# Diagonal blocks fetched by transfers, key and value banks evacuated by ScalarE, and the block inversion placed two projections later in a one-core encoder layer

## The chip, the core and the metric

The kernel runs on one core of a Trainium2 chip. The core has five instruction queues that run beside each other: PE (matrix products, with its weight loads PEld), DVE (vector engine), ACT (scalar engine: copies, exponentials and other table functions), POOL (GpSimd) and SP, which here only issues DMA transfers. Each queue is in order; engines wait for each other by semaphores. The metric is the device time of one execution in microseconds, lower is better.

## What is computed

One encoder layer on 1024 tokens of width 1024, in float32:

```python
xn = _rmsnorm(h, norm_mix_w[l])
proj = xn @ w_in[l]
q_a, k_a, v_a, qkv_g, z_g, a_g, b_g = jnp.split(proj, SPLIT_POINTS, axis=-1)
attn = _windowed_gqa(q_a, k_a, v_a, band_bias, in_window, attn_sink[l])   # 8 heads, 2 key/value heads
gdn = _gdn_mixer(qkv_g, z_g, a_g, b_g, conv_w[l], ...)                    # 4 heads, both directions
h = h + jnp.concatenate([attn, gdn], axis=-1) @ w_out[l]
h = h + jnp.square(jax.nn.relu(_rmsnorm(h, norm_ffn_w[l]) @ w_ffn_in[l])) @ w_ffn_out[l]
```

Inside the gated delta rule, each chunk, head and direction needs the inverse of a unit triangular matrix built of key products, decays and a factor:

```python
a_mat = jnp.where(strict, beta[..., :, None] * kk * decay, 0.0)
t_mat = lax.linalg.triangular_solve(eye + a_mat, jnp.broadcast_to(eye, a_mat.shape), left_side=True, lower=True)
```

The kernel uses chunks of 128 tokens, so there are 8 chunks, 4 heads and 2 directions, 64 matrices of 128 x 128.

## The kernel before

Every large product is done as three matmuls of 128 x 128 by 128 x 512 (`mm3`, L134): each operand is split into a high part (a cast on ACT, L123) and a low part (a subtraction, on POOL as a rule, L124). A projection of 128 output columns for 512 tokens is one `gemm` (L267): 24 matmuls into one of the four PSUM banks of the tag psA. `pair` (L273) walks two column tiles by two token halves, and splits the weights of a tile just ahead of its first use.

The program is written as generators. `weave` (L56) merges two streams by the costs that they yield; the order of the program is then handed to a scheduler which gives each engine its queue. An instruction traced inside `issue_after(x)` (or `behind([...])`) is put behind x, if it runs on x's engine. Tiles come from pools by tag: pg (24 buffers), pt (12), wh and wl (3 each), sc (4), dbl (2), psB (four PSUM banks) and so on; a tile waits until the buffer that it takes is free.

The stage that the change touches is the first woven one in `phases` (L1410). One stream runs 28 projections: eight of the gated heads' values with their convolutions (`proj_conv`), eight of the gate z with a Silu on ACT (L473), four of attention's keys and values and eight of its queries (`proj_attn`). The other stream runs these steps:

- `prep` (L643): for each of 8 chunks, key products (`gg`, L650) and key by query products (`kq`, L652) on PE; for each direction the decay's exponent on PE (L657, L658), its exponential on ACT (L662), the matrix `at` on DVE (L666), the copies of its four 32 x 32 diagonal blocks into `diag` on ACT (L671, 64 in all), the store of `at` to DRAM (`atd`, L673), and the decayed query products (L674) with their store.
- `eliminate` (L678): two transposes of `diag` (L683) and 31 rounds of two operations (L692, L694) invert all 256 diagonal blocks at once, on DVE.
- `diag_blocks` (L698): four transposes on DVE (L703, L704) give `ct` and `ctt`.
- `invert` (L708) for the first two pairs of chunks: products on PE with `at` read back from DRAM (L727), first in blocks of 32 (L756, L769, L773), then of 64 (L798, L809), and copies between them on ACT (L737 for direction 0, L743, L759, L800) and DVE (L737 for direction 1, L783, L788, L812).

In `proj_attn` DVE takes each key and value bank out of PSUM (L491) and writes zeros into half of the low keys `kl` (L486). For a key bank SP issues two transfers that swap its halves of 64 partitions (L494, L495), ACT writes the high keys (L497, L498) and POOL the low ones (L499). A value bank is transposed on PE and copied by DVE (L503). A query bank is scaled by DVE (L509), split by ACT (L510) and POOL (L511), and stored.

Then `bias_table` (L533) issues 16 transfers of the relative bias from ACT's queue (L541) into buffers that the projection's operands leave. The second woven stage starts attention (`attn_scores`: products L556 and L557, the sum with the bias and the maximum on DVE L558, the exponential on ACT L570, the division L577, transposes L589) beside the inversion of the last two pairs of chunks and the scans. That inversion's 32-blocks are copied into one tile, `later`, by 16 copies on ACT (L743).

Of the kernel before, what the change touches and what calls it, by code (L numbers as in the profile page):

```python
# [17 lines left out]
P = 128  # L18
# [60 lines left out]
class Block:  # L79
# [187 lines left out]
    def gemm(self, ws, xs, pstag):  # L267
        ps = self.ps(pstag)
        for k in range(NK):
            self.mm3(ps, ws[0][:, k, :], ws[1][:, k, :], xs[k][:, 0], xs[k][:, 1], k == 0, k == NK - 1)  # L270
        return ps

    def pair(self, raws, order=None):  # L273

        ws = []
        for half in range(2):
            for i in range(2):
                if half == 0:
                    ws.append(self.split_w(raws, lambda r: r[:, :, i * P:(i + 1) * P]))
                yield i, half, self.gemm(ws[i], self.xt[half], "psA")  # L280
# [186 lines left out]
    def proj_z(self):  # L467
        nc = self.nc
        for p in range(2):
            raws = self.load_w(self.w_cols(self.io["w_in"][0], C_Z + 256 * p, 256))  # L470
            for i, half, ps in self.pair(raws):
                z = self.pt()
                nc.scalar.activation(out=z, in_=ps, func=AF.Silu)  # L473
# [3 lines left out]
    def proj_attn(self):  # L477
# [7 lines left out]
        for v, o in enumerate((up, lo)):  # L485
            nc.vector.tensor_copy(out=self.kl[v][o, :], in_=self.zero[o, :].to_broadcast([64, SEQ]))  # L486
        self.va = self.pg((P, NT, P))
        for i, half, ps in self.pair(raws):
            tok = slice(half * HALF, (half + 1) * HALF)
            t = self.pt()  # L490
            self.taken = nc.vector.tensor_copy(out=t, in_=ps).ins  # L491
            if i == 0:
                swap = self.pt()
                nc.sync.dma_start(out=swap[up, :], in_=t[lo, :])  # L494
                nc.sync.dma_start(out=swap[lo, :], in_=t[up, :])  # L495
                for v, (r, o) in enumerate(((lo, up), (up, lo))):
                    nc.scalar.copy(out=self.kh[v][r, tok], in_=t[r, :])  # L497
                    nc.scalar.copy(out=self.kh[v][o, tok], in_=swap[o, :])  # L498
                    nc.gpsimd.tensor_tensor(out=self.kl[v][r, tok], in0=t[r, :], in1=self.kh[v][r, tok].bitcast(F32),  # L499
                                            op=ALU.subtract)  # L500
            else:
                pv = self.transposed(t, 0)
                nc.vector.tensor_copy(out=self.va[:, 4 * half:4 * half + 4, :], in_=pv)  # L503
            yield 5.2
        for kv in range(2):
            raws = self.load_w(self.w_cols(w, C_AQ + 256 * kv, 256))
            for i, half, ps in self.pair(raws):
                q, qh = self.pt(), self.pt(dt=F32R)
                self.taken = nc.vector.tensor_scalar(out=q, in0=ps, scalar1=0.125, scalar2=None, op0=ALU.mult).ins  # L509
                self.copied_q.append(nc.scalar.copy(out=qh, in_=q).ins)  # L510
                nc.gpsimd.tensor_tensor(out=q, in0=q, in1=qh.bitcast(F32), op=ALU.subtract)  # L511
# [131 lines left out]
    def prep(self):  # L643
        nc = self.nc
        self.diag = [self.pg((P, 32, 32)) for _ in range(2)]
        for c in range(NT):
            sl = slice(c * P, (c + 1) * P)
# [5 lines left out]
            for d in range(2):  # L653
# [15 lines left out]
                for q in range(4):  # L669
                    r = slice(32 * q, 32 * q + 32)  # L670
                    nc.scalar.copy(out=self.diag[d][r, :, 4 * c:4 * c + 4].rearrange("p i h -> p h i"),  # L671
                                   in_=at[r, :, r])
                nc.sync.dma_start(out=self.atd[c, :, d], in_=at)  # L673
                nc.vector.tensor_tensor(out=dec, in0=dec, in1=kq, op=ALU.mult)  # L674
# [3 lines left out]
    def eliminate(self):  # L678
# [3 lines left out]
        for d in range(2):  # L682
            nc.vector.transpose(out=m[:, d].rearrange("p a b -> p b a") if d else m[:, d], in_=self.diag[d])  # L683
# [23 lines left out]

    def invert(self, tt, steps):  # L708
# [10 lines left out]
        for i in steps:  # L719
            ns = slice(8 * i, 8 * i + 8)  # L720
            at = []
            if i == 2:
                later = self.wl((P, 2, 8, 64), F32)
            both = self.dbl((P, 2, 2, GH, P))
            for d in range(2):
                a = both[:, d]
                nc.sync.dma_start(out=a, in_=self.atd[2 * i:2 * i + 2, :, d].rearrange("c p h x -> p c h x"))  # L727
# [11 lines left out]
            def pieces(t64, ns):  # L739
                for d in range(2):  # L740
                    for q in sub[d]:
                        c = slice(32 * (q % 2), 32 * (q % 2) + 32)
                        nc.scalar.copy(out=t64[blk(q), :, c], in_=ct[d][blk(q), :, ns].rearrange("p x n -> p n x"))  # L743

# [3 lines left out]
            if i == 2:  # L748
                for j in range(2):
                    pieces(later[:, j], slice(8 * (i + j), 8 * (i + j) + 8))  # L750
            px = self.ps("psB", (P, 8, 32))
            for n in range(8):
                for j in range(2):
                    for d in range(2):
                        s, e = pairs[d][j]
                        nc.tensor.matmul(px[blk(e), n, :], at[d][blk(s), n, blk(e)], ct[d][blk(s), :, 8 * i + n],  # L756
# [757 lines left out]
```

## Time and profile before

| | us |
|---|---|
| median of 3 runs (lowest, highest) | 1209.62 (1207.96, 1210.77) |
| the profiled execution | 1209.66 |
| its span, first to last instruction | 1207.9 |
| PE, DVE, ACT and POOL busy in the span | 1170.3, 855.2, 611.1, 560.2 |
| mean granted clock of PE | 0.993 |

Busy times are those of instructions; waiting, and issuing a DMA, do not count. An answer in order of time has the start, the time from the first to the last of the instructions merged in the line, the engine (with a q: its queue, as in a DMA's issue), the line of the kernel, the operation with its tiles, the count, and in brackets the idle time before it and what ended it. An answer of waits has the total, the count and the longest. A row of one line of the kernel has the count, the shortest, median and longest instruction in ns, and the first and last start. A row of DMA issues has the count, the size of each and the median time from issue to landing. A group of instructions has busy time, the mean ns of one, and the idle time ahead of them with what ended it.

### The profile page before, as it was taken

How to read it: one execution, taken by the hardware profiler on the slowest of the kernel's cores; microseconds unless marked ns; L12 is line 12 of the kernel's file. 1: busy time of each engine (PE TensorE's matmuls, PEld its weight loads, DVE VectorE, ACT ScalarE, POOL GpSimd, SP SyncE). 2: the span in 40 equal slices, each digit the busy share in tenths (PEclk: the TensorE clock that was granted, in tenths of full speed). 3: DMA queues.
4: the chain of work that ended last, by engine and by line, in shares of the span. 5: the costliest groups of instructions: out<-in, count | busy, mean ns of one | idle time of the engine just before them, and what ended most of it. 6: DMA issues, size and time to landing. Idle time of an engine off the chain costs nothing. (4 is left out here: it accounts for less than half of the span.)

```text
span 1207.9 us, 18456 instructions
## 1 busy us (share of the span) xinstructions
PE 1170.3 (97%) x6482; PEld 958.9 (79%) x6482; DVE 855.2 (71%) x1484; ACT 611.1 (51%) x1332; POOL 560.2 (46%) x469
## 2 busy tenths in 40 slices
PE   6999999899989999999999999999999999999997
PEld 5788878687768778888888888888878888888885
DVE  4676667894299996687864545454588896987976
ACT  6455597425475752134755545454646444344443
POOL 5354211234422235143856354454546565555695
PEclk9999999899999999999999999999999999999999
DMA  6124344533555567323253444444789535443323
GB/s 248 53 92 144 93 162 161 174 117 103 202 183 163 180 215 265 130 89 123 64 176 136 157 143 153 140 151 158 246 290 304 185 105 174 131 159 113 105 88 139
DMA packets 121773, 187.62 MB, mean 155 GB/s; under 512 B 11059, under 2 KB 64432, under 8 KB 121681
## 3 DMA queue, kind: packets, MB, share of 16 engines
q1 hardware_dynamic: 104020, 155.20, 39.1%
q10 hardware_dynamic: 17661, 31.24, 6.8%
q8 instruction: 51, 0.84, 0.3%
q14 instruction: 41, 0.34, 0.1%
HBM read 122.39 MB, written 63.49 MB: 154 GB/s over the span
## 5 line engine op out<-in xcount | busy, mean ns | idle before, releaser
L136 PE MATMUL psA<-pg,wh 128*128 128x512 f32 x416 | 165.2, 398 | 2.1 <-ACT pt L473 2.1
L138 PE MATMUL psA<-pg,wl 128*128 128x512 f32 x416 | 164.7, 396 | 0.0
L137 PE MATMUL psA<-pg,wh 128*128 128x512 f32 x416 | 164.3, 395 | 0.0
L124 POOL TENSOR_TENSOR wl<-wr,wh 128x512 fp32r<-128x512 f32 x44 | 66.7, 1537 | 157.2 <-ACT wh L123 127.9
L1247 DVE TENSOR_TENSOR pg<-pg 128x512 fp32r<-128x512 f32 x112 | 124.4, 1146 | 11.8 <-ACT pg L1246 11.8
L124 POOL TENSOR_TENSOR wh<-wr,wh 128x512 fp32r<-128x512 f32 x32 | 47.4, 1499 | 137.1 <-ACT wh L123 137.1
L1158 ACT ACTIVATE pt<-pt 128x512 f32<-128x512 f32 x64 | 40.3, 632 | 122.7 <-DVE pt L1148 122.7
L136 PE MATMUL psA<-pg,pg 128*128 128x512 f32 x256 | 98.9, 392 | 0.9 <-DVE pg L1294 0.9
L137 PE MATMUL psA<-pg,pg 128*128 128x512 f32 x256 | 99.4, 391 | 0.1
L138 PE MATMUL psA<-pg,pg 128*128 128x512 f32 x256 | 99.2, 389 | 0.0
L136 PEld LDWEIGHTS psA<-pg,wh 128*128 128x128 f32 x416 | 78.8, 189 | 19.5 <-ACT pt L473 2.4
L137 PEld LDWEIGHTS psA<-pg,wh 128*128 128x128 f32 x416 | 78.8, 189 | 18.1 <-issue 0.9
L138 PEld LDWEIGHTS psA<-pg,wl 128*128 128x128 f32 x416 | 78.7, 189 | 16.8
L124 POOL TENSOR_TENSOR pg<-wr,pg 128x512 fp32r<-128x512 f32 x48 | 73.1, 1555 | 38.9 <-ACT pg L123 38.9
L1246 ACT CAST pg<-pg 128x512 fp32r<-128x512 f32 x112 | 66.8, 621 | 39.3 <-DMA pg<-sd 33.1
L137 PE MATMUL psB<-pg,pg 128*128 128x512 f32 x192 | 74.9, 390 | 0.8 <-POOL pg L124 0.7
L136 PE MATMUL psB<-pg,pg 128*128 128x512 f32 x192 | 74.7, 389 | 0.0
L138 PE MATMUL psB<-pg,pg 128*128 128x512 f32 x192 | 74.7, 389 | 0.0
L1148 DVE TENSOR_TENSOR pt<-psB,pt 128x512 f32<-128x512 f32 x39 | 26.9, 690 | 59.8 <-PE psB L138 41.3
L123 ACT CAST wh<-wr 128x512 fp32r<-128x512 f32 x76 | 43.6, 623 | 48.0 <-PE psA L137 27.7
L1148 DVE TENSOR_TENSOR pt<-psA,pt 128x512 f32<-128x512 f32 x39 | 26.7, 689 | 49.4 <-PE psA L138 33.8
L136 PEld LDWEIGHTS psA<-pg,pg 128*128 128x128 f32 x256 | 48.2, 188 | 12.3 <-DVE pg L1294 2.2
(405 smaller groups left out, 3231.5 us busy)
## 6 DMA issues: line engine op xcount, KB each, us to landing
sd<-pt ACTq DMA_DIRECT2D x112, 256.0 KB, 2.1
pg<-sd SPq DMA_DIRECT2D x112, 256.0 KB, 2.8
wr<-in_w_ffn_in SPq DMA_DIRECT2D x32, 512.0 KB, 3.7
wr<-in_w_in SPq DMA_DIRECT2D x22, 512.0 KB, 5.2
pg<-in_x SPq DMA_DIRECT2D x16, 512.0 KB, 6.1
wr<-in_w_ffn_out SPq DMA_DIRECT2D x16, 512.0 KB, 4.6
sc<-kvd SPq DMA_DIRECT2D x14, 512.0 KB, 4.7
kvd<-pt SPq DMA_DIRECT2D x16, 256.0 KB, 2.5
```

The costliest lines, as they stand in the source:

```text
L123: a = nc.scalar.copy(out=h, in_=raw)
L124: b = (eng or nc.gpsimd).tensor_tensor(out=l, in0=raw, in1=h.bitcast(F32), op=ALU.subtract)
L136: nc.tensor.matmul(ps, wh, xh, start=first, stop=False, skip_group_check=onto)
L137: nc.tensor.matmul(ps, wh, xl, start=False, stop=False, skip_group_check=onto)
L138: return nc.tensor.matmul(ps, wl, xh, start=False, stop=last, skip_group_check=onto)
L1148: self.added = self.nc.vector.tensor_tensor(out=out, in0=in0, in1=in1, op=ALU.add).ins
L1158: self.nc.scalar.activation(out=c, in_=c, func=AF.Relu)
L1246: nc.scalar.copy(out=s[:, 0], in_=raw)
L1247: v.tensor_tensor(out=s[:, 1], in0=raw, in1=s[:, 0].bitcast(F32), op=ALU.subtract)
```

## The change

- The store `atd` has direction and partition outermost. The diagonal blocks of chunks 0 to 5 are fetched from it by 16 DMAs, eight ahead of chunk 5 (chunks 0 to 3) and eight ahead of chunk 7 (chunks 4 and 5). Those of chunk 6 are still copied by ACT, those of chunk 7 are moved by eight DMAs straight out of `at`. `diag` has its two inner axes exchanged, so both transposes read with a stride; they are put behind the last L674.
- ACT evacuates the key and value banks, transposed values and all, fills the zeros and issues the swaps. The low keys are subtracted on POOL behind the split of a query. The first weight split of this part is put behind the first Silu.
- The stream of the inversion gets a step of cost 24 ahead of it, which moves it in program order, and its first products are put behind the last matmul of the projection traced before them (`projected`).
- The 16 copies into `later` move ahead of the bias transfers, with an Exp of one column behind a query's split, which brings the Exp table.

```diff
     def gemm(self, ws, xs, pstag):
...
-            self.mm3(ps, ws[0][:, k, :], ws[1][:, k, :], xs[k][:, 0], xs[k][:, 1], k == 0, k == NK - 1)
+            m = self.mm3(ps, ws[0][:, k, :], ws[1][:, k, :], xs[k][:, 0], xs[k][:, 1], k == 0, k == NK - 1)
+        self.projected = m.ins
...
-    def pair(self, raws, order=None):
+    def pair(self, raws, after=()):
...
-                    ws.append(self.split_w(raws, lambda r: r[:, :, i * P:(i + 1) * P]))
+                    with self.behind(() if i else after):
+                        ws.append(self.split_w(raws, lambda r: r[:, :, i * P:(i + 1) * P]))
...
     def proj_attn(self):
...
-        for v, o in enumerate((up, lo)):
-            nc.vector.tensor_copy(out=self.kl[v][o, :], in_=self.zero[o, :].to_broadcast([64, SEQ]))
+        late = []
         self.va = self.pg((P, NT, P))
-        for i, half, ps in self.pair(raws):
+        for i, half, ps in self.pair(raws, self.gated[:1]):
...
-            self.taken = nc.vector.tensor_copy(out=t, in_=ps).ins
+            copied = nc.scalar.copy(out=t, in_=ps)
             if i == 0:
                 swap = self.pt()
-                nc.sync.dma_start(out=swap[up, :], in_=t[lo, :])
-                nc.sync.dma_start(out=swap[lo, :], in_=t[up, :])
+                nc.scalar.dma_start(out=swap[up, :], in_=t[lo, :])
+                nc.scalar.dma_start(out=swap[lo, :], in_=t[up, :])
+                late.append((t, tok))
+                if half == 0:
+                    with self.tc.issue_after(copied.ins):
+                        for v, o in enumerate((up, lo)):
+                            nc.scalar.copy(out=self.kl[v][o, :], in_=self.zero[o, :].to_broadcast([64, SEQ]))
...
-                nc.vector.tensor_copy(out=self.va[:, 4 * half:4 * half + 4, :], in_=pv)
+                nc.scalar.copy(out=self.va[:, 4 * half:4 * half + 4, :], in_=pv)
...
-                nc.gpsimd.tensor_tensor(out=q, in0=q, in1=qh.bitcast(F32), op=ALU.subtract)
+                low = nc.gpsimd.tensor_tensor(out=q, in0=q, in1=qh.bitcast(F32), op=ALU.subtract)
+                if late:
+                    t, tok = late.pop(0)
+                    for v, r in enumerate((lo, up)):
+                        with self.tc.issue_after(low.ins):
+                            nc.gpsimd.tensor_tensor(out=self.kl[v][r, tok], in0=t[r, :],
+                                                    in1=self.kh[v][r, tok].bitcast(F32), op=ALU.subtract)
...
     def prep(self):
...
+            if c in (5, NT - 1):
+                a, b = (0, 4) if c == 5 else (4, 6)
+                for d in range(2):
+                    for q in range(4):
+                        r = slice(32 * q, 32 * q + 32)
+                        nc.sync.dma_start(out=self.diag[d][r, 4 * a:4 * b, :],
+                                          in_=self.atd[d, r, a:b, :, r].rearrange("p c h x -> p (c h) x"))
...
-                for q in range(4):
+                nc.sync.dma_start(out=self.atd[d, :, c], in_=at)
+                for q in range(4 if c > 5 else 0):
                     r = slice(32 * q, 32 * q + 32)
-                    nc.scalar.copy(out=self.diag[d][r, :, 4 * c:4 * c + 4].rearrange("p i h -> p h i"),
-                                   in_=at[r, :, r])
-                nc.sync.dma_start(out=self.atd[c, :, d], in_=at)
-                nc.vector.tensor_tensor(out=dec, in0=dec, in1=kq, op=ALU.mult)
+                    if c == 6:
+                        nc.scalar.copy(out=self.diag[d][r, 4 * c:4 * c + 4, :], in_=at[r, :, r])
+                    else:
+                        nc.sync.dma_start(out=self.diag[d][r, 4 * c:4 * c + 4, :], in_=at[r, :, r])
+                self.decayed = nc.vector.tensor_tensor(out=dec, in0=dec, in1=kq, op=ALU.mult).ins
...
     def eliminate(self):
...
-            nc.vector.transpose(out=m[:, d].rearrange("p a b -> p b a") if d else m[:, d], in_=self.diag[d])
+                nc.vector.transpose(out=m[:, d].rearrange("p a b -> p b a") if d else m[:, d],
+                                    in_=self.diag[d].rearrange("p x i -> p i x"))
...
+    def pieces_behind(self):
+        self.later = self.wl((P, 2, 8, 64), F32)
+        for i in range(2):
+            self.pieces(self.later[:, i], 2 + i)
+        with self.tc.issue_after(self.copied_q[-4]):
+            self.nc.scalar.activation(out=self.small((P, 1), 1, "table"), in_=self.eps, func=AF.Exp)
...
     def invert(self, tt, steps):
...
+                        with self.behind([self.projected] if i == 0 else []):
+                            nc.tensor.matmul(px[blk(e), n, :], at[d][blk(s), n, blk(e)], ct[d][blk(s), :, 8 * i + n],
+                                             start=True, stop=True)
...
     def phases(self):
...
-                  (chain(self.prep(), self.eliminate(), self.diag_blocks(), self.invert(tt, (0, 1))), 100.0)))
+                  (chain(self.prep(), self.eliminate(), self.diag_blocks(), iter((24.0,)),
+                         self.invert(tt, (0, 1))), 100.0)))
+        self.pieces_behind()
         self.bias_table()
```

`pieces` is the former inner function of `invert`, now a method with the same copies.

More of the change, by code (lines that the diff above doesn't have):

```diff
@@ L472, in proj_z @@
                 z = self.pt()
-                nc.scalar.activation(out=z, in_=ps, func=AF.Silu)
+                self.gated.append(nc.scalar.activation(out=z, in_=ps, func=AF.Silu).ins)
                 nc.sync.dma_start(out=self.zd[2 * p + i, :, half * HALF:(half + 1) * HALF], in_=z)
@@ L681, in eliminate @@
         m, t = self.dbl((P, 2, 32, 32)), self.dbl((P, 2, 32, 32))
-        for d in range(2):
-            nc.vector.transpose(out=m[:, d].rearrange("p a b -> p b a") if d else m[:, d], in_=self.diag[d])
+        with self.tc.issue_after(self.decayed):
+            for d in range(2):
+                nc.vector.transpose(out=m[:, d].rearrange("p a b -> p b a") if d else m[:, d],
+                                    in_=self.diag[d].rearrange("p x i -> p i x"))
         nc.gpsimd.memset(t.rearrange("p d a b -> p (d a b)"), 0.0)
@@ L706, in diag_blocks, with pieces @@
             yield 2.4
+    def pieces(self, t64, i):
+        for d, sub in enumerate(((0, 1), (3, 2))):
+            for q in sub:
+                r, c = slice(32 * q, 32 * q + 32), slice(32 * (q % 2), 32 * (q % 2) + 32)
+                self.nc.scalar.copy(out=t64[r, :, c],
+                                    in_=self.ct[d][r, :, 8 * i:8 * i + 8].rearrange("p x n -> p n x"))
+    def pieces_behind(self):
[4 more added lines that the diff above has]
+            self.nc.scalar.activation(out=self.small((P, 1), 1, "table"), in_=self.eps, func=AF.Exp)
     def invert(self, tt, steps):
@@ L726, in invert @@
                 a = both[:, d]
-                nc.sync.dma_start(out=a, in_=self.atd[2 * i:2 * i + 2, :, d].rearrange("c p h x -> p c h x"))
+                nc.sync.dma_start(out=a, in_=self.atd[d, :, 2 * i:2 * i + 2])
                 at.append(flat(a))
@@ L737, in diagonal @@
                     nc.vector.tensor_copy(out=out, in_=src) if d else nc.scalar.copy(out=out, in_=src)
[L739 to L743, printed above, removed]
             if i == 2:
@@ L776, in invert @@
                 t64 = self.pt((P, 8, 64))
-                pieces(t64, ns)
+                self.pieces(t64, i)
             else:
-                t64 = later[:, i - 2]
+                t64 = self.later[:, i - 2]
             for d in range(2):
@@ L802, in invert @@
             if i < 2:
-                with self.behind([self.taken]):
+                with self.behind(self.taken):
                     diagonal(1)
```

15 lines of the change are left out of this document (4 added, 11 removed).

## The prediction, made before the change was run

> **What bounds the kernel now.** I read the page first, then the waits of PE, then the windows and the order of time where PE waits. The profiled execution took 1209.66 us, 1.8 us of it outside the span, and its span is
>
> ```profile
> span 1207.9 us, 18456 instructions
> ...
> PE 1170.3 (97%) x6482; PEld 958.9 (79%) x6482; DVE 855.2 (71%) x1484; ACT 611.1 (51%) x1332; POOL 560.2 (46%) x469
> ```
>
> PE is the bound: it is idle for 1207.9 - 1170.3 = 37.6 us. An edit pays only where PE waits or runs at a lower clock, and costs only where it makes PE wait. The waits of PE from 144 to 222 us, the stage in which `prep` runs beside the projections (the longest three), and from 325 to 345 us, the start of attention (the longest two):
>
> ```profile
> PE psB L424 <- DVE pt L674: 1.7, 1, 1.7
> PE psB L652 <- ACT pt L662: 0.6, 1, 0.6
> PE psB L424 <- ACT pt L662: 0.6, 2, 0.4
> ```
>
> ```profile
> PE psB L769 <- ACT pt L759: 1.9, 1, 1.9
> PE psA L589 <- DVE wr L577: 1.2, 1, 1.2
> ```
>
> The windows give the clock of the place where the first ones lie (columns: length, then busy us of PE, PEld, DVE, ACT, POOL, then the granted clock):
>
> ```profile
> 210.00:220.00 10.00, 7.39 (x46) 5.46 (x45) 8.16 (x17) 9.79 (x27) 6.64 (x5) 1.00 0.75 238
> 220.00:230.00 10.00, 7.85 (x24) 6.13 (x23) 9.15 (x18) 3.70 (x6) 0.98 (x2) 0.66 0.80 279
> ```
>
> ACT is busy for 9.79 of 10 us, PE is idle for 2.61 + 2.15 = 4.76 us in these 20 us, and the second ten run at a mean clock of 0.66. PE in order of time, round the hole:
>
> ```profile
> 214.31 0.39 PE L137 MATMUL psA<-pg,wh 128*128 128x512 f32 x1
> 214.54 0.39 PE L138 MATMUL psA<-pg,wl 128*128 128x512 f32 x1
> ...
> 222.31 0.80 PE L136 MATMUL psA<-pg,wh 128*128 128x512 f32 x1 [2.15 <-ACT pt L473]
> ...
> 227.60 0.51 PE L136 MATMUL psA<-pg,wh 128*128 128x512 f32 x1
> ```
>
> At full clock one projection matmul follows the next by 0.23 us (first two rows). From 222.31 to 227.60, 12 of them take 5.29 us, where 12 x 0.23 = 2.76 were due: 2.53 us lost to the clock, behind a hole whose own idle time is 4.76 us. And ACT, which ends the hole:
>
> ```profile
> 213.92 2.18 ACT L662 ACTIVATE pt<-psB,ngc 128x128 f32<-128x128 f32 x8
> 215.94 1.66 ACT L671 COPY pg<-pt 32x128 f32<-32x128 f32 x4
> 217.63 1.14 ACT L123 CAST wh<-wr 128x512 fp32r<-128x512 f32 x2
> 218.67 1.68 ACT L671 COPY pg<-pt 32x128 f32<-32x128 f32 x4
> 220.37 1.28 ACT L473 ACT_TABLE_LOAD   x1
> 221.66 0.60 ACT L473 ACTIVATE pt<-psA 128x512 f32<-128x512 f32 x1
> ```
>
> The Silu of the first gate projection (L473), which frees the PSUM bank that PE waits for, stands behind the exponentials, two groups of diagonal copies (L671), a weight cast (L123) and its table load. ACT's queue is the cause, not PE's work.
>
> **The diagonal copies become transfers.** All the copies are
>
> ```profile
> L671 ACT COPY pg<-pt x64: 398/418/438, 148.2 to 219.9; 32x128 f32<-32x128 f32 x64
> ```
>
> Chunk 6 keeps 8 of 64. 56 x 0.418 = 23.4 us leave ACT. What that is worth is read at the hole. Behind the last exponential (213.92 + 2.18 = 216.1) the two groups of copies (1.66 + 1.68) and the cast (1.14, put behind the first Silu by the new edge in `pair`) go; the Silu's table load starts at about 216.1 and the first Silu ends near 216.1 + 1.28 + 0.60 = 218.0, where it ended near 222.3. That is 4.3 us at the least, with no operation of an earlier chunk moved. Earlier chunks lose their copies too, so the exponentials come earlier as well and the 0.6 us at L652 goes. Upper bound: all of 0.64 + 4.76, plus 2.53 of the clock, 7.9 us. What is late next is DVE's L674, which frees the PSUM banks of the four groups of transposes (L424); for that I keep 1.0 us of idle time. I take -6.9 us. From below: -4.3 if the clock falls as before.
>
> On this the Trainium skill, page "TensorE: Matmul & The Clock Gate", Part 1, has a rule: a window of about 3.4 us of idle PE halves the clock. The longest wait here is 2.15 us, and the clock fell all the same; by the page's Part 4 transposes do not count as busy in the same way, and from the last projection matmul to the next there are 7.8 us. By that reading a hole of 3.4 us is still enough, and the sum would be 2.5 us worse.
>
> **The transfers themselves.** 24 DMAs of 128-byte runs join SP's queue: eight ahead of chunk 5 (512 runs each), eight ahead of chunk 7 (256), eight of chunk 7 itself out of SBUF (128). Behind them on SP stand the writes of the later chunks and the next weight loads, none of which PE needs for some ten us. The first two batches wait for writes that landed chunks ago. Only the last lie on a path, that of the elimination. For their landing the nearest rows:
>
> ```profile
> pt<-pt SPq DMA_DIRECT2D x4, 128.0 KB, 4.6
> ...
> wr<-in_w_in SPq DMA_DIRECT2D x1, 64.0 KB, 4.8
> ```
>
> An SBUF to SBUF transfer lands after 4.6 us, one with 1024 runs of 64 bytes after 4.8 us. I take 4.7, from 2.5 to 8. The page "DMA: Bandwidth & Descriptors" of the Trainium skill (Specifications) says that runs under 512 bytes miss the line rate; the 4.8 us row, with shorter runs than any here, shows no long delay, so the term stays.
>
> The elimination on DVE now:
>
> ```profile
> 220.38 1.91 DVE L683 STREAM_TRANSPOSE dbl<-pg 128x1024 f32<-128x1024 f32 x1 [0.93 <-ACT pg L671]
> 222.39 0.26 DVE L692 TENSOR_TENSOR pt<-dbl,dbl 128x62 f32<-128x62 f32 x1
> 222.56 2.47 DVE L464 TENSOR_TENSOR pt<-psB,irk 128x512 f32<-128x512 f32 x4
> ...
> 265.72 2.06 DVE L704 STREAM_TRANSPOSE sc<-dbl 128x1024 f32<-128x1024 f32 x1
> ```
>
> From 222.3 to 267.8 it takes 45.5 us, and the inversion begins at its end. With the last chunk's blocks (DVE has them near 217) landed at 221.7, and two transposes that now both read with a stride (2.06 each, the row of L704; 1.9 at the least, twice 2.06 at the most), it ends near 221.7 + 4.1 + 45.5 = 271.3; 3.5 us later than before. At its old place PE would arrive 6.9 us earlier, at 260.9, and wait 10.4 us. Two projections are 48 x 0.23 = 11.0 us: PE arrives at 271.9. So this move hides the transfers, with 0.6 us to spare, up to 3.1 where the 2.47 us of L464 lie ahead of the elimination, and more if `prep` as a whole ends earlier, which ACT's 23.4 us permit. The first products are tied to the last matmul of that projection (`projected`), so nothing pulls them ahead. Cost 0; without the cover a us per us.
>
> **Keys and values on ACT.** DVE loses four PSUM copies, two zero fills and two value copies, ACT gains them: 6 x 0.60 (the Silu row: the same size out of PSUM) and two fills of at most 1.3 each, some 6 us, and the four swap transfers' issue. They fall from 240 to 270, where ACT idles:
>
> ```profile
> L123 ACT CAST wh<-wr 128x512 fp32r<-128x512 f32 x10 | 5.7, 619 | 27.5 <-PE psA L137 22.6 <-PE psA L138 4.9
> ```
>
> That is 27.5 us of idle time ahead of ten weight casts between 230 and 310 us, so they cost nothing. Before, these copies stood behind the elimination on DVE; four PSUM banks hid it up to 267.7. Behind ACT's wait for the swap (4.6 us) stand the next bank's copy and a weight cast; PE has three more banks, 16 us. The low key halves move on POOL behind a query's split: nobody needs them before attention. Cost 0 (from -1 to +1).
>
> **Inversion, copies and Exp table ahead of the bias.** ACT at the end of this stage:
>
> ```profile
> 309.77 6.10 ACTq L541 DMA_DIRECT2D pg<-biasd  x10
> 315.97 0.62 ACT L510 CAST pt<-pt 128x512 fp32r<-128x512 f32 x1 [5.70 <-DMA pg<-biasd]
> 315.99 5.04 ACTq L541 DMA_DIRECT2D pg<-biasd  x6
> ...
> 326.32 3.24 ACT L743 COPY wl<-sc 32x256 f32<-32x256 f32 x5
> 329.59 0.62 ACT L510 CAST pt<-pt 128x512 fp32r<-128x512 f32 x1
> 330.11 0.36 ACT L759 COPY pt<-psB 128x256 f32<-128x256 f32 x1
> 330.49 1.28 ACT L570 ACT_TABLE_LOAD   x1
> ```
>
> Issuing the 16 bias transfers holds ACT's queue for 6.10 + 5.04 = 11.1 us; then come 16 copies for the later inversion (0.65 each, 10.4 us), and only then L759, for which PE waits 1.9 us, and the Exp table, whose lateness shows as the 1.2 us at L589. Copies and table put ahead give back at most 3.1 us. But two projections' worth of inversion copies, 16 of 0.65, now fall into the same stretch. I take the middle of 0 and -3.1: -1.5.
>
> **Sum.** -6.9 - 1.5 = -8.4 against 1209.66; the runs' median, 1209.62, is 0.04 below. **1201.2 us.** A measurement of this kernel tells 0.2% (2.4 us) from no change: faster is below 1207.2, slower above 1212.0.
>
> **Rivals.** *The clock falls all the same*, as the hole stays long enough: 1201.2 + 2.5 = 1203.7. For it: the clock fell behind no wait over 2.15 us. Against: the hole shrinks by 4.3 us at least.
>
> *The transfers or the elimination are late*, and PE waits for `ct` at the inversion: with a landing of 8 us (3.3 more) and transposes of twice 2.06 us (4.1 more) the elimination ends at 278.7, PE waits 6.8 us, and the clock drops once more (2.5): 1210.5. No change that can be told.
>
> *ACT becomes the bound under the last three projections* (the slower side). The bias tiles come free only as the second last pair is consumed (309.77 is the first issue). If the 16 copies (10.4 us), the table (1.3) and the second inversion step (eight copies of 0.65 and two evacuations, 6.2) all stand between that point and the 11.1 us of issue, with two query splits (1.2), the last issue ends 30.2 us after it, at 340.0 on the old clock of events, and has landed at 344.7. PE stood ready for its next work at 330.1 - 1.9 = 328.2, to which at most one projection's time (5.5) of that inversion step is added: 333.7. PE waits 11.0 us in place of 3.1, and with the clock once more (2.5) the time is 1209.66 - 6.9 + 11.0 - 3.1 + 2.5 = 1213.2. It decides from the point at which the copies begin after the first bias issue; begun before, they lie in idle time.
>
> *The order does not change*: the hole is DVE's, L674 ends it. Then the 0.64 and at most 2 us of the waits at L424 go: 1207.0.
>
> **How the numbers follow.** Forecast (1197 to 1203) 0.56, clock 0.17, late elimination 0.09, unchanged order 0.05, ACT the bound 0.13. Low end: all bounds at once, 1209.66 - 7.9 - 3.1 = 1198.7, less some 3 us if attention, which then starts earlier, loses its next waits too: 1195.5. The high end takes in the late elimination: 1210.5. Only the late elimination lies within 0.2%, only ACT as the bound above it. Faster 0.78, within 0.2% 0.09, slower 0.13.
>
> **What would show it.** L671 with 8 copies; no wait of PE over 1 us from 210 to 225 and a granted clock of 1.00 there; the first Silu before 218; the first L683 some 5 us after the last decay matrix; the first L756 without a wait for DVE or a DMA; L759 of the third inversion step at once behind its products. Wrong would be: a clock under 0.9 in that window, PE waiting for L704, or ACT's bias issue at the end of the projections with PE or DVE waiting for it.

## The result, and the profile after

| | us |
|---|---|
| before, median of 6 runs (lowest, highest) | 1209.53 (1207.55, 1210.77) |
| after, median of 6 runs (lowest, highest) | 1201.04 (1198.60, 1202.83) |
| ratio after to before, 95% interval | 0.9925 [0.9912, 0.9937] |
| profiled execution after, and its span | 1199.80, 1198.0 |

The forecast was 1201.2 us. The profiled execution is 1.2 us below the median of its kernel, so what follows adds up to 9.9 us, and the medians differ by 8.5. The page of the changed kernel, its span and the line of busy times:

```profile
span 1198.0 us, 18430 instructions
...
PE 1166.0 (97%) x6482; PEld 955.6 (80%) x6482; DVE 858.9 (72%) x1476; ACT 593.9 (50%) x1285; POOL 558.8 (47%) x469
```

The span is 9.9 us shorter. PE's idle time is 1198.0 - 1166.0 = 32.0 us where it was 37.6, and its 6482 matmuls are busy for 4.3 us less. ACT lost only 17.2 us of work. The windows of the changed kernel over the place of the hole (columns as in the prediction):

```profile
210.00:220.00 10.00, 10.00 (x57) 8.20 (x56) 5.56 (x11) 6.66 (x15) 3.57 (x5) 1.00 0.68 210
220.00:230.00 10.00, 10.00 (x46) 8.29 (x45) 8.42 (x16) 1.20 (x2) 1.04 (x1) 1.00 0.58 190
```

PE is busy all through, at a granted clock of 1.00 in both (before 7.39 and 7.85 of 10 us, the second at 0.66). ACT has 6.66 us of work where it had 9.79. PE and ACT of the changed kernel in order of time:

```profile
213.85 2.11 PE L426 MATMUL psB<-ident,sc 128*128 128x128 f32 x16
215.72 0.47 PE L136 MATMUL psA<-pg,wh 128*128 128x512 f32 x1
```

```profile
211.37 2.18 ACT L680 ACTIVATE pt<-psB,ngc 128x128 f32<-128x128 f32 x8 [2.33 <-issue]
213.56 1.28 ACT L476 ACT_TABLE_LOAD   x1
214.86 1.58 ACT L476 ACTIVATE pt<-psA 128x512 f32<-128x512 f32 x3
```

The transposes run into the third gate projection without a wait. Its first matmul starts at 215.72, before at 222.31: 6.6 us. From 140 us up to this matmul PE was idle for 5.4 us before and is idle for none now. The other 1.2 us are busy time of the same 412 matmuls: before, the last 16 transposes stood apart in four groups of 0.66 us, and now they run on end in 2.11. ACT's last exponentials are followed at once by the Silu's table load, and three Silus run together from 214.86. From this matmul to the last of eight projections (192 matmuls, start to start) PE took 46.0 us before and takes 43.9 now, and 0.4 us of the 43.9 are transposes of a value bank, which stood elsewhere before. So the clock gave 2.5 us more: 9.1 in all.

The waits of PE in the changed kernel from 215 to 330 us:

```profile
PE psB L784 <- DMA dbl<-atd: 2.1, 2, 1.1
PE psA L600 <- DVE wr L588: 1.0, 1, 1.0
```

The first is new. The inversion's first products wait for `at`, which is read back from DRAM; before, PE waited 0.7 us in all in the inversion beside the projections. The clock falls there too, as the same window shows, first of the kernel before, then of the changed one:

```profile
270.00:280.00 10.00, 9.54 (x180) 7.60 (x182) 3.94 (x8) 8.33 (x14) 6.18 (x8) 1.00 0.33 107
```

```profile
270.00:280.00 10.00, 7.91 (x86) 6.11 (x86) 5.80 (x5) 4.40 (x8) 3.92 (x4) 0.83 0.66 223
```

The projections end 7.1 us earlier than before (318.01 against 325.14), the first transposes of attention's probabilities 9.3 us (327.72 against 337.02), the scans' first products (L875, before L847) 9.5 us. So the account is about -9 at the hole, +2 at the inversion, with its clock, and -2 at the start of attention. The rest of the program is as long as it was, within 0.4 us.

### The profile page after: what moved, and what is told of

Read it like the earlier page. It is cut to its first block, busy times and chain, and to the rows that moved or that the text cites. A ratio compares the mean times of both kernels' runs of the same rounds, so it can differ in the third digit from the quotient of the medians.

```text
span 1198.0 us, 18430 instructions
## 1 busy us (share of the span) xinstructions
PE 1166.0 (97%) x6482; PEld 955.6 (80%) x6482; DVE 858.9 (72%) x1476; ACT 593.9 (50%) x1285; POOL 558.8 (47%) x469
## 5 line engine op out<-in xcount | busy, mean ns | idle before, releaser
L136 PEld LDWEIGHTS psA<-pg,wh 128*128 128x128 f32 x416 | 78.5, 189 | 17.2
L1274 ACT CAST pg<-pg 128x512 fp32r<-128x512 f32 x112 | 67.2, 620 | 38.7 <-DMA pg<-sd 32.3
```

The lines of the kernel that those rows point to most:

```text
L136: nc.tensor.matmul(ps, wh, xh, start=first, stop=False, skip_group_check=onto)
L1274: nc.scalar.copy(out=s[:, 0], in_=raw)
```

## The experiments

Each is compared with the kernel before on the same chip. Where two experiments are compared, it is by their medians; the kernel before has medians from 1208.9 to 1210.1 us on the chips used, so 1 us between two experiments on different chips tells nothing.

**The transfers taken back.** All 64 diagonal blocks are copied by ACT, in the new layout, and nothing else is changed.

```diff
-            if c in (5, NT - 1):
...
-                for q in range(4 if c > 5 else 0):
+                for q in range(4):
...
-                    if c == 6:
-                        nc.scalar.copy(out=self.diag[d][r, 4 * c:4 * c + 4, :], in_=at[r, :, r])
-                    else:
-                        nc.sync.dma_start(out=self.diag[d][r, 4 * c:4 * c + 4, :], in_=at[r, :, r])
+                    nc.scalar.copy(out=self.diag[d][r, 4 * c:4 * c + 4, :], in_=at[r, :, r])
```

> The changed kernel with all 64 groups of diagonal copies on ACT again (in the new layout of diag), no transfers for them. Theory (the hole at the end of prep was ACT's queue of diagonal copies): with 0.29 us each, as the eight that were left took in the changed kernel's trace, some 19 us go back to ACT, the last chunk's eight ahead of the first Silu are 2.4 us, earlier chunks' copies add to it; the hole comes back by 3 to 5 us and the clock may drop (2.5): 1204 to 1208 us. Rival (the weight split put behind the first Silu, or the bank copies on ACT, closed the hole): no wait of PE over 1 us from 210 to 225, 1200 to 1202.

Measured: 1201.55 us (1198.30 to 1202.81), ratio 0.9922 [0.9893, 0.9951]. My theory fell: the transfers bring nothing to the total. The group of copies, the wait at the hole and the window of this kernel:

```profile
L683 ACT COPY pg<-pt 32x128 f32<-32x128 f32 x64 | 18.9, 295 | 4.2 <-DVE pt L677 3.6
```

```profile
PE psA L136 <- ACT pt L476: 1.8, 1, 1.8
```

```profile
220.00:230.00 10.00, 10.00 (x46) 8.26 (x45) 9.43 (x21) 1.88 (x5) 2.54 (x2) 1.00 0.70 238
```

A copy takes 295 ns, where it took 418 in the kernel before: the change also exchanged the inner axes of `diag`, so that a copy writes one contiguous run in each partition. A hole of 1.8 us is left and the third gate projection starts at 218.70, 3.0 us later than with the transfers, but the clock stays at 1.00. On the other side the elimination starts earlier, and PE finds everything ready at the inversion: the 2.1 us are not there.

**The old layout.** The same kernel with the old order of `diag`'s axes:

```diff
-                    nc.scalar.copy(out=self.diag[d][r, 4 * c:4 * c + 4, :], in_=at[r, :, r])
+                    nc.scalar.copy(out=self.diag[d][r, :, 4 * c:4 * c + 4].rearrange("p i h -> p h i"), in_=at[r, :, r])
...
-                                    in_=self.diag[d].rearrange("p x i -> p i x"))
+                                    in_=self.diag[d])
```

> As e1_copies_back (all diagonal copies on ACT), but with the old order of the two inner axes of diag, so that a copy writes with a stride (0.42 us each before, 0.30 in e1) and the first transpose reads without one. Theory now (what closed the hole in e1 is that 64 copies became 0.12 us cheaper, 8 us less of ACT): ACT is later by some 2.5 us at the first Silu, PE's wait there 4 us, with the half clock behind it: 1204 to 1207 us. Rival (the edge and the order of the transposes closed it, not the copies' length): 1200.5 to 1203.

Measured: 1205.92 us (1204.68 to 1209.18), ratio 0.9972 [0.9955, 0.9989]. The theory held. Its group, wait and window:

```profile
L683 ACT COPY pg<-pt 32x128 f32<-32x128 f32 x64 | 26.8, 418 | 4.2 <-DVE pt L677 3.6
```

```profile
PE psA L136 <- ACT pt L476: 2.7, 1, 2.7
```

```profile
220.00:230.00 10.00, 8.68 (x31) 7.03 (x32) 9.57 (x17) 4.46 (x8) 2.51 (x2) 0.83 0.77 264
```

26.8 - 18.9 = 7.9 us more on ACT, the hole is 2.7 us, the clock falls to 0.83, and the time is 4.4 us above that of the kernel with the new layout (6.0 by the two ratios, each to the kernel before on its own chip). The opposite pair, the transfers with the old layout, was not run.

**The layout alone.** The kernel before, with nothing but the two lines above turned round.

> The kernel before with the new layout of the diagonal blocks alone: ScalarE's 64 copies write contiguous runs, and the elimination's two transposes read with strides. Theory (a shorter copy is what opens the hole's cure; the inversion at its old place then waits for the elimination): 64 x 0.12 us = 7.9 us leave ScalarE, first Silu some 4 to 6 us earlier, the clock kept at 1.00 in 210 to 230; TensorE reaches the inversion some 6 us earlier and waits there for the elimination, so that most of it is given back: 1205 to 1208. Rival (the layout alone is worth what it was worth in the changed kernel, 4.4 us or more, and nothing waits): 1202 to 1205. Rival 2 (nothing comes of it): 1209 to 1210.

Measured: 1208.01 us (1205.34 to 1209.38), ratio 0.9993 [0.9984, 1.0003]. Nothing that can be told from no change, as rival 2 had it, though by the mechanism of none of the three: ACT was relieved, and DVE took its place. The waits of PE, then DVE and POOL in order of time, in this kernel:

```profile
PE psB L424 <- DVE pt L666: 2.6, 1, 2.6
PE psB L424 <- DVE pt L673: 1.8, 1, 1.8
```

```profile
210.24 4.12 DVE L486 CAST pg<-zero 64x1024 fp32r<-64x1024 f32 x2 [1.28 <-PE psB L652]
214.29 1.36 DVE L666 SCALAR_TENSOR_TENSOR pt<-pt,cc,psB 128x128 f32<-128x128 f32 x5
...
216.94 1.95 DVE L682 STREAM_TRANSPOSE dbl<-pg 128x1024 f32<-128x1024 f32 x1
218.83 0.63 DVE L673 TENSOR_TENSOR pt<-pt,psB 128x512 f32<-128x512 f32 x1
```

```profile
209.08 2.99 POOL L124 TENSOR_TENSOR wl<-wr,wh 128x512 fp32r<-128x512 f32 x2 [21.99 <-ACT wh L123]
212.01 1.80 POOL L683 MEMSET dbl<- 128x2048 f32 x1
```

In the kernel before, DVE fills the zeros of the low keys (L486) just ahead of the last chunk's matrices (L666), and does the elimination's first transpose (here L682) ahead of the last decayed query products (here L673). The first wait above is behind the fills, the second behind the transpose. The change gives the fills to ACT, behind a key bank, and puts the transposes behind the last L674. So the hole had two causes, ACT's copies and DVE's order of work, and the change takes both away. The prediction worked out the first alone, and kept 1.0 us for the last L674 without saying what held it.

**The edge behind the first Silu.** The kernel with all copies on ACT in the new layout, without the edge that puts a weight split behind the Silu:

```diff
-        for i, half, ps in self.pair(raws, self.gated[:1]):
+        for i, half, ps in self.pair(raws):
```

> As e1_copies_back, without the edge that puts the first weight split of the keys behind the first Silu. If that edge is what closed the hole, the split's two casts (1.1 us) come ahead of the Silu again, and PE waits 3 us in place of 1.8, with or without the half clock (2.5): 1202.5 to 1205.5 us. Rival (the copies' length alone): within 1 us of e1, 1200.5 to 1202.5.

Measured: 1201.28 us (1200.69 to 1203.04), ratio 0.9933 [0.9920, 0.9947]. The hole grows to 2.9 us and the clock falls to 0.83 from 220 to 230, but the elimination starts earlier and meets only two pairs of POOL's weight splits in place of three or four. The edge is worth nothing that can be told in the time.

**The inversion at its old place.**

```diff
-                        with self.behind([self.projected] if i == 0 else []):
+                        with self.behind([]):
...
-                  (chain(self.prep(), self.eliminate(), self.diag_blocks(), iter((24.0,)),
-                         self.invert(tt, (0, 1))), 100.0)))
+                  (chain(self.prep(), self.eliminate(), self.diag_blocks(), self.invert(tt, (0, 1))), 100.0)))
```

> The changed kernel with the inversion at its old place in the order: neither the step of cost 24 nor the edge to the last projection matmul. Theory: the elimination ends at 274.6 and PE is at the old place near 261, so PE waits 11 to 13 us there and the clock drops once (2.5); the wait of 2.1 us for the matrices read back goes: 1211 to 1215 us. Rival (the move is not needed, as the scheduler finds projections to put ahead of it): 1200 to 1203.

Measured: 1218.28 us (1216.87 to 1220.41), ratio 1.0064 [1.0042, 1.0087], slower than the kernel before. The direction held, the size did not. The wait of PE at the inversion in this kernel:

```profile
PE psB L784 <- DMA dbl<-atd: 11.7, 2, 10.8
```

The prediction had 10.4 us for it. The rest of the 17.2 us against the changed kernel is in the clock and at the start of attention, as far as one profiled execution (1220.41 us) tells: the granted clock is 0.50 from 270 to 280 (0.83 in the changed kernel) and 0.66 from 340 to 350 (1.00). The projections end 14.3 us later than in the changed kernel (332.31), the scans' first products start 19.9 us later (367.92).

**The inversion later still**, with 28 units in place of 24:

```diff
-                  (chain(self.prep(), self.eliminate(), self.diag_blocks(), iter((24.0,)),
+                  (chain(self.prep(), self.eliminate(), self.diag_blocks(), iter((28.0,)),
```

> The changed kernel with the inversion four units later in the order (28 in place of 24). Theory (the 2.1 us that TensorE waits at the inversion for the blocks read back goes, but the inversion's last products then stand later among the first scores, and TensorE waits there): 1201 to 1205, with the wait at the start of attention grown by 2 us or more. Rival (the wait goes and nothing comes in its place): 1198.5 to 1199.5.

Measured: 1208.31 us (1207.37 to 1209.97), ratio 1.0000 [0.9991, 1.0009]: worse than the theory allowed. The 2.1 us at the inversion are gone. The waits that came, from 215 to 345 us in this kernel:

```profile
PE psA L567 <- DMA pt<-qad: 4.0, 1, 4.0
PE psA L612 <- ACT pt L602: 3.1, 1, 3.1
```

The second half of the second inversion step, which has the last projection to lie beside in the changed kernel, now stands among the first scores. PE comes to these 7.5 us earlier (310.39 against 317.85), waits 4.0 us for a query that is still on its way through DRAM, and runs at a clock of 0.66 from 320 to 330. Of the three places tried, that of the change is the best: 17.2 us are lost with the whole step taken out, 7.3 with four units more. Places between were not run.

**Key and value banks back on DVE** (the fills stay on ACT):

```diff
-            copied = nc.scalar.copy(out=t, in_=ps)
+            copied = nc.vector.tensor_copy(out=t, in_=ps)
...
-                nc.scalar.copy(out=self.va[:, 4 * half:4 * half + 4, :], in_=pv)
+                nc.vector.tensor_copy(out=self.va[:, 4 * half:4 * half + 4, :], in_=pv)
```

> The changed kernel with the four key and value banks and the transposed values copied by DVE, as before; zeros, swaps and low keys stay as changed. Theory (these copies have to leave DVE once the elimination ends after PE has filled four banks): DVE gets to them at 274.6, PE has filled the last bank near 260 and waits 13 us or so, clock once more 2.5: 1212 to 1217 us. Rival (cost 0 as in the prediction, both sides hidden): 1200 to 1203.

Measured: 1208.01 us (1206.33 to 1211.75), ratio 0.9985 [0.9969, 1.0000]. Smaller than expected, and by another mechanism than full banks. The wait in this kernel:

```profile
PE psB L426 <- DVE pt L493: 7.6, 2, 7.4
```

PE's queue is in order, and the transposes of a value bank need its copy, which stands in DVE's queue behind the elimination; every projection behind them waits too. Before, the first value transposes stood behind the inversion's first step, at 280.26, when the elimination was over. This edit costs nothing only because ACT makes the copies: 7.0 us hang on it.

**Inversion copies and Exp table back behind the bias.**

```diff
+            if i == 2:
+                self.later = self.wl((P, 2, 8, 64), F32)
...
+                for j in range(2):
+                    self.pieces(self.later[:, j], 2 + j)
...
-        self.pieces_behind()
```

> The changed kernel with the copies into later and the Exp table where they were, behind the bias. Theory (they made PE wait at the start of attention): the wait for L759's copy, near 1.9 us, comes back, with some half clock: 1202.5 to 1205 us. Rival (the bias or DVE is the limit there anyway): 1200 to 1202.

Measured: 1202.20 us (1200.85 to 1204.61), ratio 0.9932 [0.9907, 0.9958]. That is 1.2 us above the changed kernel, and the intervals overlap widely: inconclusive. The profiled execution, the slowest of the five, has a wait of 1.3 us at L600 in place of 1.0, and takes 32.3 us from the end of the projections to the scans' first products, where the changed kernel takes 30.0 and the kernel before 32.4; the clock is 0.83 from 340 to 350.

**POOL beside the elimination.** In the changed kernel the elimination ends at 274.6, where 271.3 was forecast. Its rounds, as groups of the kernel before and of the changed kernel:

```profile
L692 DVE TENSOR_TENSOR pt<-dbl,dbl 128x62 f32<-128x62 f32 (+15 forms) x31 | 17.3, 559 | 1.1
L694 DVE TENSOR_TENSOR dbl<-dbl,pt 128x62 f32<-128x62 f32 (+15 forms) x31 | 17.3, 559 | 1.0
```

```profile
L714 DVE TENSOR_TENSOR pt<-dbl,dbl 128x62 f32<-128x62 f32 (+15 forms) x31 | 20.3, 655 | 1.1
L716 DVE TENSOR_TENSOR dbl<-dbl,pt 128x62 f32<-128x62 f32 (+15 forms) x31 | 20.3, 654 | 1.0
```

The same 62 operations take 40.6 us in place of 34.6. POOL and DVE of the changed kernel in order of time:

```profile
232.87 2.89 POOL L124 TENSOR_TENSOR wl<-wr,wh 128x512 fp32r<-128x512 f32 x2 [11.83 <-ACT wh L123]
238.31 3.37 POOL L124 TENSOR_TENSOR wl<-wr,wh 128x512 fp32r<-128x512 f32 x2 [2.55 <-ACT wh L123]
```

```profile
232.42 0.56 DVE L716 TENSOR_TENSOR dbl<-dbl,pt 128x384 f32<-128x384 f32 x1
233.01 1.59 DVE L714 TENSOR_TENSOR pt<-dbl,dbl 128x414 f32<-128x414 f32 x1
234.64 1.57 DVE L716 TENSOR_TENSOR dbl<-dbl,pt 128x414 f32<-128x414 f32 x1
236.24 0.62 DVE L714 TENSOR_TENSOR pt<-dbl,dbl 128x440 f32<-128x440 f32 x1
```

Two weight splits on POOL, two long operations on DVE, and their neighbours have their usual length. Four such pairs fall into the elimination now (232.87, 238.31, 255.28, 260.56), one did before (242.36): 6 more operations, each about 1 us longer. To test it, six operations on POOL were added inside the rounds:

```diff
+        pa, po = self.pt(), self.pt()
+        nc.gpsimd.memset(pa, 0.0)
...
+            if k in (15, 18, 21):
+                nc.vector.tensor_copy(out=pa[:, 0:1], in_=t[:, 0, k + 1, 0:1])
+                for _ in range(2):
+                    if k == 15:
+                        nc.gpsimd.tensor_tensor(out=po, in0=pa, in1=pa, op=ALU.subtract)
+                    elif k == 18:
+                        nc.gpsimd.tensor_scalar(out=po, in0=pa, scalar1=2.0, scalar2=None, op0=ALU.mult)
+                    else:
+                        nc.gpsimd.tensor_copy(out=po, in_=pa)
```

> The changed kernel with six operations of 128x512 added on POOL inside the elimination, two behind each of three rounds: subtractions of two tiles, then products with a constant (one tile read), then copies (one tile read). Theory (a weight split on POOL beside the elimination stretches DVE's operations: in the changed kernel eight of them take 1.5 to 1.6 us in place of 0.5 to 0.7): behind the first round about two DVE operations of 0.7 us take 1.7; behind the others as well if any read of POOL does it, or not if only two reads do. The elimination ends 2 to 6 us later and PE waits that much longer at the inversion: 1203 to 1209 us. Rival (the stretch comes of the DMA traffic or of ACT's casts that run at the same time): no operation of DVE over 0.8 us there, 1201 us.

Measured, in one execution: 1204.21 us. POOL and DVE at the added pair of two-input operations:

```profile
246.76 2.86 POOL L723 TENSOR_TENSOR pt<-pt 128x512 f32<-128x512 f32 x2 [10.52 <-DVE pt L720]
```

```profile
246.60 0.68 DVE L716 TENSOR_TENSOR pt<-dbl,dbl 128x510 f32<-128x510 f32 x1
247.31 1.41 DVE L718 TENSOR_TENSOR dbl<-dbl,pt 128x510 f32<-128x510 f32 x1
248.76 1.40 DVE L716 TENSOR_TENSOR pt<-dbl,dbl 128x504 f32<-128x504 f32 x1
250.20 0.69 DVE L718 TENSOR_TENSOR dbl<-dbl,pt 128x504 f32<-128x504 f32 x1
```

Each POOL operation lengthens one DVE operation: by 0.7 us where it has two inputs, by 0.3 where it has one (the pairs of tensor_scalar and of copies gave 0.95 and 0.93, then 0.88 and 0.85, where 0.56 to 0.66 were due); POOL's memset beside the rounds lengthened none. So the mechanism is shown. The time of this kernel does not measure it, for other things moved too: PE's wait at the inversion grew from 2.1 to 3.3 us, but PE also waits 1.6 us for a Silu at 234.38, which the changed kernel does not.

**The last chunk's blocks behind the first Silu.** ACT copies them, so that neither the transfers' landing nor ACT's copies ahead of the Silu stand on a path.

```diff
-                for q in range(4 if c > 5 else 0):
...
-                    else:
-                        nc.sync.dma_start(out=self.diag[d][r, 4 * c:4 * c + 4, :], in_=at[r, :, r])
+                elif c > 6:
+                    last.append(at)
...
+        while not self.gated:
+            yield 0.5
+        with self.tc.issue_after(self.gated[0]):
+            for d in range(2):
+                for q in range(4):
+                    r = slice(32 * q, 32 * q + 32)
+                    nc.scalar.copy(out=self.diag[d][r, 4 * NT - 4:4 * NT, :], in_=last[d][r, :, r])
```

> The changed kernel, but the blocks of chunk 7 are copied by ACT, behind the first Silu, and not by eight transfers. Theory (the transfers of chunk 7 delay the elimination by their issue one after the other on SP and their landing, 217.3 and 221.05 for the two transposes where DVE had the blocks at 213 and 214.5; this costs the 2.1 us for which PE waits at the inversion): the elimination starts some 2 us earlier, that wait goes to under 0.5 us, and the hole stays closed: 1198.5 to 1200 us. Rival (that wait is hidden, or the copies delay the next Silus): 1201 or more.

Measured: 1204.41 us (1202.28 to 1205.38), ratio 0.9952 [0.9939, 0.9964]. The hole is closed and the elimination ends 3.4 us earlier, but the loop's costs also moved the inversion by one projection, so that this run tells two things at once. The next one takes five units off the 24:

```diff
-                  (chain(self.prep(), self.eliminate(), self.diag_blocks(), iter((24.0,)),
+                  (chain(self.prep(), self.eliminate(), self.diag_blocks(), iter((19.0,)),
```

> Chunk 7's eight diagonal blocks are copied by ScalarE behind the first Silu, and the inversion's place in the order is that of the changed kernel (five units taken off the 24, against the five that the loop that waits for the Silu puts in). Theory (the hole ahead of the gate's third projection and the elimination's late start each cost 2 to 3 us, and this edit ends both): no wait over 1 us at the hole, elimination ended at about 271, no wait of TensorE for the blocks read back at the inversion, 1198.0 to 1200.0. Rival (the 2.1 us at the inversion is given back at the start of attention, where TensorE waits for the divisions and the Exp): 1200.5 to 1202.5. If the shifted inversion was not what cost the earlier run its 3 us, 1204 again.

Measured: 1201.41 us (1199.11 to 1202.81), ratio 0.9938 [0.9926, 0.9949]; the rival held. No wait for the blocks read back is left, and PE comes to the first scores 4.4 us earlier than in the changed kernel (313.50 against 317.85). Yet the scans' first products start at 347.92, in the changed kernel at 348.05. All of it is given back at the start of attention. PE's longest wait there, the window, and one line's DVE and POOL operations in this kernel:

```profile
PE psA L599 <- DVE wr L587: 2.3, 2, 1.9
```

```profile
320.00:330.00 10.00, 6.62 (x56) 5.30 (x54) 9.84 (x29) 5.51 (x19) 3.72 (x4) 0.81 0.17 49
```

```profile
L587 DVE TENSOR_SCALAR wr<-wr,nm x3: 336/427/2322, 322.0 to 324.6; 128x256 f32<-128x256 f32 x3
```

```profile
322.73 1.84 POOL L774 MEMSET pg<- 128x1024 f32 x2
```

DVE is busy for 9.84 of 10 us. One of three divisions took 2322 ns, where the shortest took 336, just as POOL wrote two memsets; in the changed kernel those run from 320.80, beside other DVE operations, and its three divisions take 334 to 411 ns. That the memsets held the division is read from this trace; no run was made without them.

**Half of the last chunk's transfers.** The blocks of the second direction are copied by ACT:

```diff
-                    if c == 6:
+                    if c == 6 or d == 1:
```

> Chunk 7's four blocks of the second direction are copied by ScalarE (4 x 0.29 us) in place of four transfers; those of the first direction stay transfers. Theory (the elimination waits for the last transfers, which SyncE issues one after the other): the second transpose no longer waits for a transfer, the elimination ends 1.5 to 2.5 us earlier, and the first Silu comes 1.2 us later; TensorE's 2.1 us at the inversion shrink by the one and grow by the other: 1199.5 to 1201.5. Rival (the added 1.2 us opens the hole and drops the clock): 1203 or more.

Measured: 1200.06 us (1198.63 to 1203.89), ratio 0.9936 [0.9922, 0.9950]. Both of PE's waits moved as the theory had it: 1.8 us at the hole, at a clock of 1.00, and none at the inversion. The transposes in this kernel run at 215.47, both together, where the second started at 221.05 in the changed kernel, and the elimination's last transpose ends some 2.4 us earlier. The time can't be told from that of the changed kernel. So no version here is faster than the changed one by more than these runs can tell.

## Why the prediction was right, step by step

The forecast of 1201.2 us is 0.2 from the median, and part of that is luck: the hole gave 2.2 us more than its term, and the inversion, put at nothing, took 2.0.

**The hole** was read rightly, as ACT's queue ahead of the first Silu, and came out at -9.1 where -6.9 was forecast, beyond the upper bound of 7.9. The idle time (5.4 us) and the clock (2.5) came out as they were read. Two things were missed. The 1.0 us kept for DVE's L674 was not there, because the change also takes the fills off DVE and puts the elimination's transposes behind the last L674; the layout run on the kernel before shows what DVE would else have cost, 2.6 and 1.8 us. And the sum had no term for the 1.2 us by which the same matmuls are busy for less when they run on end. The rival on the clock did not come at the hole; the clock fell at the inversion.

But the gain does not hang on the edit to which the prediction gave it. It counted 56 copies that leave ACT, at 0.418 us each, and passed over the new layout, which alone makes a copy 0.295 us. With that layout, the other edits and no transfer at all the time is the same. The transfers close the hole's last 1.8 us and pay it back at the inversion. Whether they would have done as much with the old layout stays open.

**The transfers** were to cost nothing, with 0.6 us to spare. Here the step failed: PE waits 2.1 us, the clock falls behind it (0.83 from 270 to 280), and of the 9.1 us gained at the hole 7.1 are left at the end of the projections. The start of the rounds was better than forecast, 223.36 against 221.7 + 4.1 = 225.8, since the first transpose runs while the second direction's transfers are on their way. SP's issue and DVE in order of time in the changed kernel:

```profile
213.31 2.66 SPq L693 DMA_DIRECT2D pg<-pt  x4
217.13 2.54 SPq L693 DMA_DIRECT2D pg<-pt  x4
```

```profile
217.33 2.12 DVE L704 STREAM_TRANSPOSE dbl<-pg 128x1024 f32<-128x1024 f32 x1 [2.08 <-DMA pg<-pt]
221.05 2.21 DVE L704 STREAM_TRANSPOSE dbl<-pg 128x1024 f32<-128x1024 f32 x1 [1.60 <-DMA pg<-pt]
```

The 4.7 us taken for a landing were the wrong row: these land after 2.0 us, and what counts is that SP issues four in 2.6 us and has other work between the batches. The 45.5 us taken for the elimination were the wrong size: 6.0 us more come from POOL's weight splits, of which four pairs fall into it in place of one. Last, the prediction had PE wait for `ct`, where it waits for `at`: the read-back takes a buffer of the tag dbl that the elimination holds until its last round, so it can be issued only at 268.32, and lands 5.0 us later. The Trainium skill, page "SBUF — State Buffer", section "Who interferes with whom", says that a DVE operation with two inputs in SBUF and a GpSimd operation that reads SBUF exclude each other; the 1.4 to 1.6 us above agree with it, and with its remark that a GpSimd operation that only writes does not disturb such a one.

**Keys and values** cost nothing, as forecast: PE has no wait over 1.1 us between 215 and 317. That they would else cost 7.0 us was not seen. The prediction thought of full banks, and it is the in-order queue of PE behind the value transposes.

**Copies and Exp table** were put at -1.5; the step from the end of the projections to the first transposed probabilities gave -2.2 (9.7 us in place of 11.9). Not all of it is this edit: the run without it takes 10.3 us for the same step. Its time is 1.2 us longer, which can't be told from nothing, so the size of this term is not shown. The third inversion step's first copy stands right behind its products (321.76), and the first Exp at 322.04 needs no table load. One number on record is wrong: `later` takes 8 copies of 0.65 us (5.2 us), not 16 and 10.4, there and in the description of the kernel. It enters only the rival with ACT as the bound, whose 1213.2 should have been 5.2 lower, 1208.0. That rival did not come: the bias transfers are issued beside ACT's copies and did not hold up its instructions as forecast for it.

**The move** hides the elimination as argued, but for the 2.1 us above, at the place where PE arrives (271.35 against the 271.9 forecast). The prediction's 10.4 us for its absence were 11.7, with a lower clock and more waits behind them.

## What to carry to other kernels

Where a queue ahead of a wait is relieved, look at the shape of its operations before the count of them: here a contiguous destination took 29% off each copy (418 to 295 ns), and with it the time was the same without the 24 transfers. Ask which engine ends the wait next, and what else the change takes off that one, since here the hole had two causes, and taking away one alone left 2.7 us of it or more. And where work is moved, look at what runs on POOL beside it: the same 62 DVE operations were 6 us longer for having other neighbours.

## What the runs showed of the hardware

Time in which POOL holds a DVE operation up is counted as DVE's busy time (40.6 us in place of 34.6 for the same 62 operations), so the page shows 858.9 us of DVE after against 855.2 before, though fills and bank copies were taken off it. DVE operations with one input, from SBUF to SBUF, look held by POOL's memset too, which two-input operations were not: the division of 2322 ns in place of 336, and in the layout run one fill of 3397 ns, where the other took 691, beside a weight split and the memset right behind it. No run was made to test this by itself.

The clock does not go by the longest wait alone. From the end of the second gate projection to the third, with transposes in between, the gap was 7.4 us (before; clock 0.66 in 220 to 230), 7.3 (the layout alone, 0.75), 6.3 (old layout, 0.83), 5.2 (without the edge, 0.83), 4.2 (copies on ACT, 1.00), 3.7 (half of the transfers, 1.00) and 1.7 (after, 1.00). The Trainium skill, page "TensorE: Matmul & The Clock Gate", Part 1, has an idle window of about 3.4 us, free-running. PE fills part of these gaps with transposes, and no run here shows the window itself. Nor do the gaps give one limit: at the changed kernel's inversion 3.4 us lie between two projections (271.35 to 274.72), with waits of 1.1 and 1.0 us and 64 small products in between, and the clock was 0.83 from 270 to 280. What decides stays open.
